# Instance normalisation of 65,536 rows: row statistics by long reductions on two engines, and the last tile in two halves

## The chip, the core and the metric

The kernel runs on one core of one Trainium2 chip. The metric is the device time of one execution in microseconds (us). Executions of the kernel before lie within a few us of one another (5017.2 to 5019.7 in the first series); all runs told here are in the fast state, with a granted clock of 1.0.

Names: VectorE is DVE in the profile, ScalarE is ACT, GpSimd is POOL, and SP issues the transfers. "DMA engine" always means one of the 16 engines of the core that move data; "engine" alone is a compute engine.

## The reference

```python
x: (256, 256, 4096) float32, eps = 1e-5
mean = np.mean(x, axis=2, keepdims=True)
var = np.var(x, axis=2, keepdims=True)
return (x - mean) / np.sqrt(var + eps)
```

That is 65,536 rows of 4096 numbers: 1073.7 MB are read and as much is written.

## The kernel before

A tile is 128 partitions x 4 rows (8.4 MB); there are 128 tiles and three buffers. Each row is reduced by eight bn_stats of 512, and ScalarE normalises it in place. One queue carries loads and stores.

```python
def row(x_tile, r):
    ...
    for j in range(nsub):                       # 8 times
        nc.vector.bn_stats(out=stats[:, j, :], in_=xr[:, r, j, :])
    nc.vector.bn_aggr(out=mv, in_=stats)
    nc.scalar.activation(out=rstd, in_=mv[:, 1:2], func=Sqrt, bias=eps_tile, scale=1.0)
    nc.vector.reciprocal(out=rstd, in_=rstd)
    nc.vector.scalar_tensor_tensor(out=nbias, ...)          # -mean * rstd
    nc.scalar.activation(out=x_tile[:, r, :], in_=x_tile[:, r, :],
                         func=Identity, bias=nbias, scale=rstd)

def finish(i):
    x_tile = tiles.pop(i)
    for r in range(K):
        row(x_tile, r)
    nc.sync.dma_start(out=out_t[i], in_=x_tile)

for i in range(AHEAD):
    load(i)
for i in range(ntiles):
    finish(i)
    if i + AHEAD < ntiles:
        load(i + AHEAD)
```

Of the kernel before, what the change touches and what calls it, by code (L numbers as in the profile page):

```python
# [1 line left out]

# [4 lines left out]


@with_exitstack  # L10
def kernel(
    ctx: ExitStack,
    tc: tile.TileContext,
    x: bass.AP,
    eps: bass.AP,
    out: bass.AP,
):
    nc = tc.nc
    P = 128
    K = 4  # L20
    BUFS = 3
    AHEAD = 2

    x_flat = x.flatten_outer_dims()
    out_flat = out.flatten_outer_dims()
    n, d = x_flat.shape
    ntiles = n // (P * K)
    assert n == ntiles * P * K

    x_t = x_flat.rearrange("(t p k) d -> t p k d", p=P, k=K)  # L30
    out_t = out_flat.rearrange("(t p k) d -> t p k d", p=P, k=K)

    FMAX = nc.vector.BN_STATS_FMAX
    nsub = d // FMAX
    assert d == nsub * FMAX

    io = ctx.enter_context(tc.tile_pool(name="io", bufs=BUFS))
    small = ctx.enter_context(tc.tile_pool(name="small", bufs=8))
    singles = ctx.enter_context(tc.tile_pool(name="singles", bufs=1))

    eps_tile = singles.tile([P, 1], mybir.dt.float32)
    nc.vector.memset(eps_tile, eps)  # L42

    tiles = {}

    def load(i):
        x_tile = io.tile([P, K, d], mybir.dt.float32)
        nc.sync.dma_start(out=x_tile, in_=x_t[i])
        tiles[i] = x_tile

    def row(x_tile, r):
        xr = x_tile.rearrange("p k (s f) -> p k s f", s=nsub)
        stats = small.tile([P, nsub, 6], mybir.dt.float32)
        mv = small.tile([P, 2], mybir.dt.float32)
        rstd = small.tile([P, 1], mybir.dt.float32)
        nbias = small.tile([P, 1], mybir.dt.float32)
        for j in range(nsub):
            nc.vector.bn_stats(out=stats[:, j, :], in_=xr[:, r, j, :])  # L58
        nc.vector.bn_aggr(out=mv, in_=stats)  # L59
        nc.scalar.activation(  # L60
            out=rstd,
            in_=mv[:, 1:2],
            func=mybir.ActivationFunctionType.Sqrt,
            bias=eps_tile,
            scale=1.0,
        )
        nc.vector.reciprocal(out=rstd, in_=rstd)  # L67
        nc.vector.scalar_tensor_tensor(  # L68
            out=nbias,
            in0=mv[:, 0:1],  # L70
            scalar=-1.0,
            in1=rstd,
            op0=mybir.AluOpType.mult,
            op1=mybir.AluOpType.mult,
        )
        nc.scalar.activation(  # L76
            out=x_tile[:, r, :],
            in_=x_tile[:, r, :],
            func=mybir.ActivationFunctionType.Identity,
            bias=nbias,  # L80
            scale=rstd,
        )

    def finish(i):
        x_tile = tiles.pop(i)
        for r in range(K):
            row(x_tile, r)
        nc.sync.dma_start(out=out_t[i], in_=x_tile)

    for i in range(AHEAD):  # L90
        load(i)
    for i in range(ntiles):
        finish(i)
        if i + AHEAD < ntiles:
            load(i + AHEAD)


# [1 line left out]
_INS = ['x', 'eps']  # L99
_OUTS = [((256, 256, 4096), 'float32')]  # L100

_NUMBERS = {'eps': 9.999999747378752e-06}


# [26 lines left out]
```

## Time and profile before

| what | value | how to read it |
|---|---|---|
| time | 5017.97 us, median of 3 | profiled span 5018.0 |
| VectorE, ScalarE busy | 53%, 42% | neither is the bound |
| data queue | 99.7% of 16 DMA engines' span | transfers are the bound |
| one transfer of 8.4 MB | 19.34 us (8 packets of 2418 ns on each DMA engine) | 256 of them are 4951 us, so 67 us of the time are something else |

Columns: queue and kind, packets, MB, share of the 16 DMA engines' span.

```profile
q14 instruction: 61, 0.50, 0.0%
```

Sixty-one packets of 8 KB, rounded to 0.0%. They are the engines' own programs, fetched by the same DMA engines that move the data (the counts and packet times under "The result" show it).

### The profile page before, as it was taken

Reading aid. Unit: us, or ns where it says so; the run is one execution under the profiler, and the core shown is the slowest. Engines: PE = TensorE matmul, PEld = TensorE weight load, DVE = VectorE, ACT = ScalarE, POOL = GpSimd, SP = SyncE. Lnnn points to the kernel's source line nnn. Section 1 sums busy time; section 2 is a strip of 40 time slices with the busy share of each in tenths; the row PEclk is TensorE's granted clock in tenths of the full one; section 3 lists DMA queues with packets and bytes.
Section 4 is the critical chain, followed back from the end, with each engine's and each line's share of the span. In section 5 each row is a group of like instructions: output and inputs, shape, how many; then the busy total and the mean of one; then the engine's idle time right before and its main releaser. Section 6 shows DMA issues by size and latency. Waiting matters only on the chain.

```text
span 5018.0 us, 7844 instructions
## 1 busy us (share of the span) xinstructions
DVE 2667.3 (53%) x5633; ACT 2083.6 (42%) x1025; POOL 0.2 (0%) x4
## 2 busy tenths in 40 slices
DVE  5555455545555455554555545555455544555444
ACT  3444334443444334443344433444334443344433
POOL 0000000000000000000000000000000000000000
DMA  9999999999999999999999999999999999999998
GB/s 426 432 432 432 433 433 434 434 434 433 427 432 429 426 432 430 427 434 427 427 427 432 428 426 433 429 427 429 430 428 427 428 432 427 427 432 428 427 432 362
DMA packets 36925, 2148.00 MB, mean 428 GB/s; under 512 B 4096, under 2 KB 4096, under 8 KB 4096
## 3 DMA queue, kind: packets, MB, share of 16 engines
q1 hardware_dynamic: 36864, 2147.50, 99.7%
q14 instruction: 61, 0.50, 0.0%
HBM read 1073.74 MB, written 1073.74 MB: 428 GB/s over the span
## 4 chain that ended last, share of the span: by engine, by line
DVE 45%; another core or an unknown queue 43%; ACT 9%; DMA 1%; issue 1%; ACTq 0%
DVE stats L58 41%; ACT x_tile L76 9%; DVE mv L59 2%; DMA x_tile<-in_x_dram 1%; DVE rstd L67 1%; DVE nbias L68 1%; ACT rstd L60 1%; ACTq L60 0%
## 5 line engine op out<-in xcount | busy, mean ns | idle before, releaser
L58 DVE BATCH_NORM_STATS2 stats<-x_tile 128x6 f32<-128x512 f32 x4096 | 2506.3, 674 | 2228.2 <-DMA x_tile<-in_x_dram 2228.2
L76 ACT ACTIVATE x_tile<-x_tile,nbias,rstd 128x4096 f32<-128x4096 f32 x512 | 1945.7, 3800 | 403.5 <-DVE nbias L68 403.5
L60 ACT ACTIVATE rstd<-mv,eps_tile 128x1 f32<-128x1 f32 x512 | 148.8, 291 | 2508.5 <-DVE mv L59 2483.6
L59 DVE BATCH_NORM_AGGREGATE mv<-stats 128x2 f32<-128x48 f32 x512 | 183.7, 359 | 4.4
L67 DVE RECIPROCAL rstd<-rstd 128x1 f32<-128x1 f32 x512 | 74.8, 146 | 87.5 <-ACT rstd L60 87.3
L68 DVE SCALAR_TENSOR_TENSOR nbias<-mv,rstd 128x1 f32<-128x1 f32 x512 | 75.2, 147 | 4.3
L60 ACT ACT_TABLE_LOAD x1 | 1.3, 1283 | 0.7 <-PEq L112 0.7
L42 DVE MEMSET eps_tile<- 128x1 f32 x1 | 0.1, 59 | 0.8 <-PEq L112 0.8
L112 POOL MEMSET const-bfloat16-1.0<- 128x1 bf16 x1 | 0.1, 103 | 0.0
L112 POOL MEMSET const-uint8-127<- 128x1 uint8 x1 | 0.1, 102 | 0.0
L112 POOL MEMSET const-float32-0.0<- 128x1 f32 x1 | 0.1, 100 | 0.2 <-issue 0.2
L112 POOL MEMSET const-float32-1.0<- 128x1 f32 x1 | 0.1, 99 | 0.0
## 6 DMA issues: line engine op xcount, KB each, us to landing
x_tile<-in_x_dram SPq DMA_DIRECT2D x128, 52.3
out_dram<-x_tile SPq DMA_DIRECT2D x128, 33.3
```

The costliest lines, as they stand in the source:

```text
L42: nc.vector.memset(eps_tile, eps)
L58: nc.vector.bn_stats(out=stats[:, j, :], in_=xr[:, r, j, :])
L59: nc.vector.bn_aggr(out=mv, in_=stats)
L60: nc.scalar.activation(out=rstd, in_=mv[:, 1:2], func=mybir.ActivationFunctionType.Sqrt, bias=eps_tile, scale=1.0,)
L67: nc.vector.reciprocal(out=rstd, in_=rstd)
L68: nc.vector.scalar_tensor_tensor(out=nbias, in0=mv[:, 0:1], scalar=-1.0, in1=rstd, op0=mybir.AluOpType.mult, op1=mybir.AluOpType.mult,)
L76: nc.scalar.activation(out=x_tile[:, r, :], in_=x_tile[:, r, :], func=mybir.ActivationFunctionType.Identity, bias=nbias, scale=rstd,)
L112: nc = _bacc.Bacc("TRN2", target_bir_lowering=False, num_devices=1)
```

## The change

The intent: fewer and longer instructions for the statistics (VectorE sums a row, ScalarE sums the squares of x minus mean, both normalise), a fixed order of instructions, and a shorter end, since the last tile is loaded, computed and stored in two halves.

```diff
-        for j in range(nsub):
-            nc.vector.bn_stats(out=stats[:, j, :], in_=xr[:, r, j, :])
-        nc.vector.bn_aggr(out=mv, in_=stats)
...
+        def mean(r):
+            row = x_tile[:, r, :].rearrange("p (c f) -> p c f", c=C)      # C = 64
+            tensor_reduce(out=part[:, r, :], in_=row, op=ALU.add)
+            tensor_reduce(out=nsum[:, c], in_=part[:, r, :], op=ALU.add, negate=True)
+            tensor_scalar_mul(out=nmean[:, c], in0=nsum[:, c], scalar1=1.0 / d)
+        def square(r):
+            nc.scalar.activation(out=junk, in_=x_tile[:, r, :], func=AF.Square,
+                                 bias=nmean[:, c], scale=1.0, accum_out=ss[:, c])
+        def scales(c):    # Sqrt on ScalarE; reciprocal and nbias on VectorE
+        def apply_dve(r): # tensor_scalar(row, rstd, nbias, mult, add), 3 rows of 4
+        def apply_act(r): # activation Identity, 1 row of 4
...
-    for i in range(AHEAD):
+    spans = [(t * P * K, K) for t in range(n // (P * K) - 1)]
+    spans += [(n - P * K, K // 2), (n - P * K // 2, K // 2)]
...
+    for i in range(BUFS):
         load(i)
-    for i in range(ntiles):
-        finish(i)
-        if i + AHEAD < ntiles:
-            load(i + AHEAD)
+    for i in range(last + 1):
+        compute(i)
+        if i == last - 2:
+            load(last)
+        store(i)
+        if 1 <= i < last - 2:
+            load(i + 2)
```

More of the change, by code (lines that the diff above doesn't have):

```diff
@@ L18 @@
     nc = tc.nc
+    keep = tc.keep_in_program_order
+    fp32 = mybir.dt.float32
+    AX = mybir.AxisListType
+    AF = mybir.ActivationFunctionType
+    ALU = mybir.AluOpType
     P = 128
@@ L21 @@
     BUFS = 3
-    AHEAD = 2
+    C = 64
     x_flat = x.flatten_outer_dims()
@@ L26, with rows @@
     n, d = x_flat.shape
-    ntiles = n // (P * K)
-    assert n == ntiles * P * K
-    x_t = x_flat.rearrange("(t p k) d -> t p k d", p=P, k=K)
-    out_t = out_flat.rearrange("(t p k) d -> t p k d", p=P, k=K)
-    FMAX = nc.vector.BN_STATS_FMAX
-    nsub = d // FMAX
-    assert d == nsub * FMAX
+    assert n % (P * K) == 0 and d % C == 0
+    spans = [(t * P * K, K) for t in range(n // (P * K) - 1)]
+    spans += [(n - P * K, K // 2), (n - P * K // 2, K // 2)]
+    last = len(spans) - 1
+    def rows(flat, span):
+        r0, k = span
+        return flat[r0 : r0 + P * k, :].rearrange("(p k) d -> p k d", k=k)
@@ L37 @@
     io = ctx.enter_context(tc.tile_pool(name="io", bufs=BUFS))
-    small = ctx.enter_context(tc.tile_pool(name="small", bufs=8))
+    small = ctx.enter_context(tc.tile_pool(name="small", bufs=4))
     singles = ctx.enter_context(tc.tile_pool(name="singles", bufs=1))
-    eps_tile = singles.tile([P, 1], mybir.dt.float32)
+    psum = ctx.enter_context(tc.tile_pool(name="psum", bufs=1, space=bass.MemoryType.PSUM))
+    eps_tile = singles.tile([P, 1], fp32)
     nc.vector.memset(eps_tile, eps)
+    junk = psum.tile([P, d], fp32)
@@ L44 @@
     tiles = {}
     def load(i):
-        x_tile = io.tile([P, K, d], mybir.dt.float32)
-        nc.sync.dma_start(out=x_tile, in_=x_t[i])
+        x_tile = io.tile([P, K, d], fp32)
+        keep(nc.sync.dma_start(out=x_tile[:, : spans[i][1], :], in_=rows(x_flat, spans[i])))
         tiles[i] = x_tile
-    def row(x_tile, r):
-        xr = x_tile.rearrange("p k (s f) -> p k s f", s=nsub)
-        stats = small.tile([P, nsub, 6], mybir.dt.float32)
-        mv = small.tile([P, 2], mybir.dt.float32)
-        rstd = small.tile([P, 1], mybir.dt.float32)
-        nbias = small.tile([P, 1], mybir.dt.float32)
-        for j in range(nsub):
-            nc.vector.bn_stats(out=stats[:, j, :], in_=xr[:, r, j, :])
-        nc.vector.bn_aggr(out=mv, in_=stats)
-        nc.scalar.activation(
-            out=rstd,
-            in_=mv[:, 1:2],
-            func=mybir.ActivationFunctionType.Sqrt,
-            bias=eps_tile,
-            scale=1.0,
-        )
-        nc.vector.reciprocal(out=rstd, in_=rstd)
-        nc.vector.scalar_tensor_tensor(
-            out=nbias,
-            in0=mv[:, 0:1],
-            scalar=-1.0,
-            in1=rstd,
-            op0=mybir.AluOpType.mult,
-            op1=mybir.AluOpType.mult,
-        )
-        nc.scalar.activation(
-            out=x_tile[:, r, :],
-            in_=x_tile[:, r, :],
-            func=mybir.ActivationFunctionType.Identity,
-            bias=nbias,
-            scale=rstd,
-        )
@@ L84, in finish, with compute @@
-    def finish(i):
-        x_tile = tiles.pop(i)
-        for r in range(K):
-            row(x_tile, r)
-        nc.sync.dma_start(out=out_t[i], in_=x_tile)
-    for i in range(AHEAD):
-        load(i)
-    for i in range(ntiles):
-        finish(i)
-        if i + AHEAD < ntiles:
-            load(i + AHEAD)
+    def compute(i):
+        x_tile = tiles[i]
+        k = spans[i][1]
+        part = small.tile([P, K, C], fp32)
+        nsum = small.tile([P, K], fp32)
+        nmean = small.tile([P, K], fp32)
+        ss = small.tile([P, K], fp32)
+        std = small.tile([P, K], fp32)
+        rstd = small.tile([P, K], fp32)
+        nbias = small.tile([P, K], fp32)
+        def mean(r):
+            c = slice(r, r + 1)
+            row = x_tile[:, r, :].rearrange("p (c f) -> p c f", c=C)
+            keep(nc.vector.tensor_reduce(out=part[:, r, :], in_=row, axis=AX.X, op=ALU.add))
+            keep(nc.vector.tensor_reduce(out=nsum[:, c], in_=part[:, r, :], axis=AX.X, op=ALU.add, negate=True))
+            keep(nc.vector.tensor_scalar_mul(out=nmean[:, c], in0=nsum[:, c], scalar1=1.0 / d))
+        def square(r):
+            c = slice(r, r + 1)
+            keep(
+                nc.scalar.activation(
+                    out=junk, in_=x_tile[:, r, :], func=AF.Square, bias=nmean[:, c], scale=1.0, accum_out=ss[:, c]
+                )
+            )
+        def scales(c):
+            keep(nc.scalar.activation(out=std[:, c], in_=ss[:, c], func=AF.Sqrt, bias=eps_tile, scale=1.0 / d))
+            keep(nc.vector.reciprocal(out=rstd[:, c], in_=std[:, c]))
+            keep(nc.vector.tensor_mul(out=nbias[:, c], in0=nmean[:, c], in1=rstd[:, c]))
+        def apply_dve(r):
+            c = slice(r, r + 1)
+            row = x_tile[:, r, :]
+            keep(
+                nc.vector.tensor_scalar(
+                    out=row, in0=row, scalar1=rstd[:, c], scalar2=nbias[:, c], op0=ALU.mult, op1=ALU.add
+                )
+            )
+        def apply_act(r):
+            c = slice(r, r + 1)
+            row = x_tile[:, r, :]
+            keep(nc.scalar.activation(out=row, in_=row, func=AF.Identity, bias=nbias[:, c], scale=rstd[:, c]))
+        for r in range(k - 1):
+            mean(r)
+            square(r)
+        mean(k - 1)
+        scales(slice(0, k - 1))
+        square(k - 1)
+        for r in range(k - 2):
+            apply_dve(r)
+        scales(slice(k - 1, k))
+        apply_dve(k - 1)
+        apply_act(k - 2)
@@ L99, with store @@
+    def store(i):
+        keep(nc.sync.dma_start(out=rows(out_flat, spans[i]), in_=tiles.pop(i)[:, : spans[i][1], :]))
+    for i in range(BUFS):
+        load(i)
+    for i in range(last + 1):
[5 more added lines that the diff above has]
+            load(i + 2)
 _INS = ['x', 'eps']
```

## The prediction

> **What bounds the kernel now.** I began with the page: the engines' busy shares against the DMA queue's.
>
> ```profile
> DVE 2667.3 (53%) x5633; ACT 2083.6 (42%) x1025; POOL 0.2 (0%) x4
> ...
> DMA packets 36925, 2148.00 MB, mean 428 GB/s; under 512 B 4096, under 2 KB 4096, under 8 KB 4096
> ...
> q1 hardware_dynamic: 36864, 2147.50, 99.7%
> ```
>
> VectorE works for half of the span, ScalarE for less, and the one data queue for 99.7%. The best slices of the page move 434 GB/s and the last only 362, so whatever is not full speed lies mostly at the end. The page's chain of work is no help: it gives 45% to VectorE and 43% to "another core or an unknown queue", because it walks back through the statistics of a tile and doesn't see that the transfers run on beside them.
>
> Next, the timeline of one steady period, to see whether transfers wait for computing or the reverse.
>
> ```profile
> 4918.19 0.33 SPq L88 DMA_DIRECT2D out_dram<-x_tile  x1
> 4918.61 0.38 SPq L48 DMA_DIRECT2D x_tile<-in_x_dram  x1
> 4931.53 5.44 DVE L58 BATCH_NORM_STATS2 stats<-x_tile 128x6 f32<-128x512 f32 x9 [17.21 <-DMA x_tile<-in_x_dram]
> ...
> 4956.97 39.79 SPq L88 DMA_DIRECT2D out_dram<-x_tile  x2
> ```
>
> The store of a tile and the load two tiles on are issued together at 4918.2. VectorE had by then waited since 4914.3 for the next tile, which lands at 4931.5; 25.4 us later (4956.97) that tile is stored. So when computing ends, the queue still has 13 to 14 us of an older load to move. This is the slack of the kernel: a tile could take up to 13 us longer to compute before the last DMA engine ran dry. The landing times fit a queue that is served in order: 33.3 us for a store is the 14 us left over plus one transfer of 19.3 us, and 52.3 us for a load is one transfer more.
>
> Then the records of single packets. Each transfer is 8 packets of 64 KB on each of 16 engines; 29,786 of 32,768 took 2418 ns (so 19.34 us for 8), the mean is 2442 ns, and the excess is in the last packet of a transfer. The 16 completions of one transfer lie 0.5 us apart in the first transfer, 6.5 in the 21st, 12 in the 61st, and 11 to 12.7 from there on: one engine falls behind until the leading ones reach the end of their queue as the next store is issued. From transfer 60 on all need some 19.56 us a transfer. The time of the program is that of its slowest engine, 256 transfers, plus the time in which that engine has nothing to do.
>
> Where is that? Windows over the end (columns: busy time of VectorE, ScalarE and GpSimd, clock, DMA share, GB/s):
>
> ```profile
> 4976.00:4980.00 4.00, 4.00 (x10) 2.31 (x2) 0.00 (x0) 1.00 0.34 147
> 4980.00:4984.00 4.00, 4.00 (x10) 3.00 (x3) 0.00 (x0) 1.00 0.26 115
> 4984.00:4988.00 4.00, 4.00 (x9) 3.18 (x2) 0.00 (x0) 1.00 0.08 33
> 4988.00:4996.00 8.00, 3.82 (x10) 7.39 (x3) 0.00 (x0) 1.00 0.00 0
> 4996.00:5016.00 20.00, 0.00 (x0) 0.40 (x1) 0.00 (x0) 1.00 0.97 419
> ```
>
> The last tile is being computed, with nothing left to move. Most engines stop near 4978; a share of 0.08 is about one engine of 16, and the packet records have that last one finish at 4989.8. The last store is issued at 4996.4 and its first packet starts at 4997.3. So the leading engines lose 19 us, the one that counts loses 4997.3 - 4989.8 = 7.4 us.
>
> **What the Trainium skill says.** "DMA: Bandwidth & Descriptors", section "Where 436 GB/s comes from", gives a ceiling of 435.2 GB/s for a core's 16 ports; the trace agrees, with 434 in its best slices and 64 KB per 2418 ns, or 433.7 GB/s for 16. Even 2147.5 MB at 435.2 GB/s would take 4934 us, 1.7% less than now: 2% faster is out of reach for any change that moves the same bytes. The same page, section "Queues, rings and completion order", says that each DMA engine takes its descriptors in ring order; the 33.3 and 52.3 us above agree. "VectorE: DVE Perf Modes", section "The perf-mode tier table", has tensor_reduce at one element a cycle and fp32 tensor_scalar in SBUF at two (1227 ns for 2048). The kernel before has neither, so this stands untested; its bn_stats of 512 take 674 ns, one element per 1/0.96 ns plus 141 ns. "ScalarE: Activation LUTs", section "What ACT_TABLE_LOAD costs", gives 280 ns + 0.833 ns per element for an ACTIVATE with a pointer as bias and 93 ns for a second pointer: 3785 ns at 4096, where the trace has 3800.
>
> **The change, part by part.** Removed from a tile: 32 bn_stats of 674 ns, 4 aggregates, 4 square roots, 4 pairs of small operations. Added, as estimates:
> - A row's sum: one reduce of 4096, 4096/0.96 + 141 = 4.41 us; a reduce of 64, 0.21; a scaling, 0.15 (the small operations before took 0.147). With 0.04 us between dependent ones and some 0.07 overlap between free ones, 4.77 us a row, 19.1 for four.
> - Square of a row on ScalarE: 280 + 3412 = 3.69 us, four times, beside the sums of the next row. The accumulated output may add some 0.1 us.
> - Normalising a row: VectorE 1.227 + 2048/2/0.96 = 2.29 us, three rows; ScalarE 3.80, one row.
>
> VectorE: 4 x 4.77 + 3 x 2.29 + 0.6 = 26.6 us a tile (before 20.8); ScalarE 4 x 3.7 + 3.8 + 0.6 = 19.2 (before 16.3). Both stay well under the 39.2 us that the two transfers of a tile take, so all this work is beside the transfers. "Long instructions" save nothing on the path: VectorE gets more work, not less.
>
> What could touch the path is the latency of a tile. Sums end at 19.1; scales of three rows 19.5; two rows normalised 24.0; scales of the last row 24.4; last row 26.7. On ScalarE the fourth square ends at 22.9, its root at 23.3, the third row at 27.1. So 27.1 us against 25.4: the slack falls from about 14 to 12.3 us and stays positive. The store of a tile is issued 1.7 us later and the leading engines run into it at a smaller spread, some 10 instead of 12 us, so the slow phase (19.56 instead of about 19.47 us a transfer of the slowest engine) begins perhaps 20 transfers sooner: 20 x 0.09, about +2 us.
>
> The start: the built order of issues is the same in both kernels. Three loads are already issued together at 0.73 us before (the scheduler had moved the third up), then store 0, store 1, load 3. So the extra load ahead in the source changes nothing. A second table load (1.28 us, once) falls in tile 0, whose store queues behind load 2 until about 62 us anyway. Tile 1 should be done at 22.6 + 2 x 27.1 + about 2 = 79 us, just before the first store has left the queue at some 82.
>
> The end: the order becomes store 125, half load, half load, store 126, half store, half store. On the slowest engine, from the landing of tile 126: store 125 to 19.4, the halves to 29.1 and 38.8, store 126 to 58.2, half stores to 67.9 and 77.6. Tile 126 is done at 27.1; a half needs 9.5 (two sums) + 3.7 + 0.4 + 3.8 = 17.5 us, so the first half, landed at about 31, is done by 49, the second by 65 to 66. The last store thus joins a queue that is busy until 67.9: no gap. Before, the same count gives 85.4. Saved: about 7.5 us, which is the gap of 7.4 measured above.
>
> Sum: 5018.0 - 7.4 + 2 = about 5012; I put 5011, since the earlier slow phase is the softest term.
>
> **The rivals.** First, VectorE's normalisation runs at one element a cycle, 4.41 us. Then a tile takes 33 us and the slack is about 6. Steady state would still be bound by transfers, but tile 1 would be done only at about 90 us, 8 us after the first store leaves the queue, the last half would be 1 to 3 us late, and the spread would hit its limit much sooner (some 8 us). Time: 5018 - 7 + 8 + 2 + 8, about 5029. For it speaks only that this trace has no such instruction; against it the table of the skill. Second, engines that run dry cost more than I count: the excess of packets goes from 3 ns a packet at 700 us to some 29 after 1250 us, as the spread reaches its limit. If a tighter slack raises it by another 10 ns, that is 2048 x 10 ns = 20 us, about 5031. Third, reading the windows as "the queue is idle from 4978 to 4997" would promise 19 us and 4999; I hold against it that the lagging engine carries its delay to the end, so that the last stores of the new kernel should end spread over several us. It would come true if shorter transfers let that engine catch up. Fourth, computing becomes the bound: it would take a tile of over 39 us, which no term gives.
>
> **Range and chances.** Most weight is on 5008 to 5016. The gap's 19 us taken whole gives the lower end, 5001; the first or second rival gives the upper, 5028. Faster by 2% (below 4917.6) is beneath the time at the port ceiling: 0.01. Slower by 2% (above 5118) needs 0.8 us more for each tile: 0.02. Within 2%: 0.97.
>
> **What would show it.** Right: the queue again at 99.7% or more; VectorE near 68% and ScalarE near 49% busy; long reduces near 4.4 us, normalisation near 2.3; a tile's store some 27 us after its landing; DMA share without a zero in windows before the last store, and completions of the last store microseconds apart. Wrong: normalisation of 4.4 us, a gap near 82 us, a share below 0.97 in middle windows, mean packets well above 2442 ns, or a last half done after the queue is empty.

## The result

The changed kernel took **4995.92 us** (median of 4: 4990.08 to 4996.78) against 5018.83 us for the kernel before in the same rounds. The ratio is 0.9952 (95% interval 0.9935 to 0.9969). Ratios here are the mean time of one kernel's fast runs over that of the other's of the same rounds, so they are not quite the ratio of the medians. The prediction was 5011, with a range down to 5001.

The page of the changed kernel, first its engines and queues:

```profile
DVE 3392.6 (68%) x2436; ACT 2501.4 (50%) x1413; POOL 0.2 (0%) x4
...
q1 hardware_dynamic: 37152, 2147.50, 99.9%
q14 instruction: 38, 0.31, 0.0%
```

VectorE works 725 us more and the kernel is faster all the same: transfers are still the bound. VectorE executes 2436 instructions instead of 5633, and the instruction queue has 38 packets in place of 61.

The costliest groups (line, engine, operation, operands, shapes, count, busy us, mean ns, idle time before them):

```profile
L74 DVE TENSOR_REDUCE part<-x_tile 128x64 f32<-128x4096 f32 x512 | 2258.8, 4412 | 1520.3 <-DMA x_tile<-in_x_dram 1520.3
...
L95 DVE TENSOR_SCALAR x_tile<-x_tile,rstd,nbias 128x4096 f32<-128x4096 f32 x383 | 912.6, 2411 | 10.4 <-DVE nbias L89 1.1
...
L81 ACT ACTIVATION_READ_ACCUMULATOR junk<-x_tile,nmean 128x1 f32 x512 | 95.5, 187 | 0.0
```

The long reduce takes 4412 ns and the normalisation 2411 ns, so VectorE does run the latter at about two elements a cycle. The accumulated output of Square costs an instruction of its own of 187 ns.

One steady period of the timeline, which answers to the one shown of the kernel before:

```profile
4862.97 0.33 SPq L118 DMA_DIRECT2D out_dram<-x_tile  x1
4863.35 0.43 SPq L57 DMA_DIRECT2D x_tile<-in_x_dram  x1
4875.38 4.42 DVE L74 TENSOR_REDUCE part<-x_tile 128x64 f32<-128x4096 f32 x1 [12.47 <-DMA x_tile<-in_x_dram]
...
4902.43 0.33 SPq L118 DMA_DIRECT2D out_dram<-x_tile  x1
```

A tile takes 4902.43 - 4875.38 = 27.05 us, where 27.1 was expected, and 12.4 us of queue are left when a store is issued.

Windows over the end (columns as in the prediction):

```profile
4940.00:4960.00 20.00, 13.73 (x12) 12.39 (x8) 0.00 (x0) 1.00 1.02 416
4960.00:4970.00 10.00, 9.83 (x9) 5.38 (x5) 0.00 (x0) 1.00 0.98 426
4970.00:4976.00 6.00, 2.00 (x4) 5.97 (x4) 0.00 (x0) 1.00 0.85 366
4976.00:4980.00 4.00, 0.81 (x1) 1.67 (x1) 0.00 (x0) 1.00 0.73 311
4980.00:4984.00 4.00, 0.00 (x0) 0.00 (x0) 0.00 (x0) 1.00 0.93 401
```

The zero of the kernel before is gone. Only the leading DMA engines pause near 4976, and the 16 completions of the last store lie 4.6 us apart. So the end went as predicted, and what is missing from the prediction came from the middle. Here are windows over the middle, first before, then after; the last two columns are the DMA share and GB/s.

```profile
250.00:1125.00 875.00, 469.78 (x994) 371.36 (x183) 0.00 (x0) 1.00 1.00 433
1125.00:2000.00 875.00, 461.63 (x974) 357.93 (x176) 0.00 (x0) 1.00 1.00 430
2000.00:3000.00 1000.00, 538.64 (x1139) 422.82 (x208) 0.00 (x0) 1.00 1.00 429
```

```profile
250.00:1125.00 875.00, 598.43 (x431) 442.54 (x251) 0.00 (x0) 1.00 1.00 433
1125.00:2000.00 875.00, 597.66 (x428) 436.36 (x246) 0.00 (x0) 1.00 1.00 434
2000.00:3000.00 1000.00, 677.37 (x486) 499.10 (x282) 0.00 (x0) 1.00 1.00 431
```

Before, the rate falls from 433 to 430 after 1125 us; after, it holds 434 until 2000. The DMA share says 1.00 throughout: a slower packet counts as a busy one.

The packet records tell where the slower packets come from. I followed the completion of the last of the 16 DMA engines from transfer to transfer and subtracted 19.32 us. Before the leaders run out of queue, this excess is zero in most transfers and jumps in a few. Each column here is a packet of the instruction queue, with the excess of the last DMA engine in the transfer during which it ran. These are the fetches in VectorE's rhythm from 491 us before and from 1117 us after, and the others from 971 us after (the rhythm is explained below):

```
before: fetch at us   491.5  601.2  720.0  836.7  953.4  1062.9
        excess us      0.66   0.71   0.78   0.78   0.76    0.78
after:  fetch at us  1116.8 1349.5 1582.3 1853.7 2086.5
        excess us      0.82   0.93   0.94   0.96   0.94
after, other fetches  971.3 1151.6 1495.1 1809.5 2156.4
        excess us      0.00   0.00   0.00   0.00   0.00
```

Before, the jumps come every 110 to 117 us, which is the time in which VectorE executes some 128 instructions; after, every 230 to 270. The fetch packet itself takes 0.31 us, and in every case the data packet that starts 0.3 us after it is 0.15 to 0.65 us longer than 2418 ns. At 720.0 us, for instance, that packet takes 2886 ns: 0.31 + 0.47 is the jump of 0.78. The others have a longer packet after them too, but on a DMA engine that isn't the last, so the excess stays zero. Three earlier fetches in VectorE's rhythm after the change (340.7, 614.2 and 845.4 us) cost only 0.32, 0.00 and 0.60 us: their DMA engine was not yet, or only just, the last one. And not every jump is a fetch: in the first 40 transfers of the changed kernel there are others of up to 1.1 us. The count fits too. The trace records 5639, 1663 and 520 instructions on VectorE, ScalarE and SP before; at 128 for a packet that is 44 + 13 + 4 = 61. After it is 2568, 1928 and 399: 20 + 15 + 3 = 38. Both are exactly the packets of the queue.

So the theory to test (F) is: **every 128 instructions of a compute engine take some 0.8 to 0.9 us from one particular DMA engine. VectorE's program always falls on the same one, which therefore becomes the last, and the last one sets the time.** Long instructions help by being few. By F, 24 or 25 fetches fewer should give some 17 us beside the 7.4 of the end. The rivals: (T) the two halves win all 19 us of idle time at the end instead of 7.4; (L) the longer latency of a tile holds the DMA engines closer together.

### The profile page after: what moved, and what is told of

Read it like the earlier page. It is cut to its first block, busy times and chain, and to the rows that moved or that the text cites. A ratio compares the mean times of both kernels' runs of the same rounds, so it can differ in the third digit from the quotient of the medians.

```text
span 4994.1 us, 4917 instructions
## 1 busy us (share of the span) xinstructions
DVE 3392.6 (68%) x2436; ACT 2501.4 (50%) x1413; POOL 0.2 (0%) x4
## 3 DMA queue, kind: packets, MB, share of 16 engines
q1 hardware_dynamic: 37152, 2147.50, 99.9%
## 4 chain that ended last, share of the span: by engine, by line
DVE 53%; DMA 23%; another core or an unknown queue 20%; ACT 3%; issue 1%; SPq 0%; ACTq 0%
DVE part L74 37%; DMA x_tile<-in_x_dram 22%; DVE x_tile L95 12%; DVE nsum L75 2%; ACT junk L81 2%; ACT x_tile L103 2%; DVE nmean L76 1%; DMA out_dram<-x_tile 1%; DVE nbias L89 1%; DVE rstd L88 0%; SPq L118 0%; ACTq L159 0%; ACT L87 0%; ACT std L87 0%
## 5 line engine op out<-in xcount | busy, mean ns | idle before, releaser
L74 DVE TENSOR_REDUCE part<-x_tile 128x64 f32<-128x4096 f32 x512 | 2258.8, 4412 | 1520.3 <-DMA x_tile<-in_x_dram 1520.3
L81 ACT ACTIVATE junk<-x_tile,nmean 128x4096 f32<-128x4096 f32 x512 | 1883.0, 3678 | 2445.2 <-DVE nmean L76 2445.2
L95 DVE TENSOR_SCALAR x_tile<-x_tile,rstd,nbias 128x4096 f32<-128x4096 f32 x383 | 912.6, 2411 | 10.4 <-DVE nbias L89 1.1
L103 ACT ACTIVATE x_tile<-x_tile,nbias,rstd 128x4096 f32<-128x4096 f32 x129 | 488.5, 3787 | 0.1
L75 DVE TENSOR_REDUCE nsum<-part 128x1 f32<-128x64 f32 x512 | 112.7, 220 | 17.7
L81 ACT ACTIVATION_READ_ACCUMULATOR junk<-x_tile,nmean 128x1 f32 x512 | 95.5, 187 | 0.0
L76 DVE TENSOR_SCALAR nmean<-nsum 128x1 f32<-128x1 f32 x512 | 78.7, 154 | 17.5
L87 ACT ACTIVATE std<-ss,eps_tile 128x3 f32<-128x3 f32 (+1 forms) x258 | 76.2, 295 | 8.3
L88 DVE RECIPROCAL rstd<-std 128x3 f32<-128x3 f32 (+1 forms) x258 | 41.6, 161 | 8.6 <-ACT std L87 8.6
L89 DVE TENSOR_TENSOR nbias<-nmean,rstd 128x3 f32<-128x3 f32 (+1 forms) x258 | 41.5, 161 | 8.9
```

Source lines behind the costliest of these rows:

```text
L74: keep(nc.vector.tensor_reduce(out=part[:, r, :], in_=row, axis=AX.X, op=ALU.add))
L75: keep(nc.vector.tensor_reduce(out=nsum[:, c], in_=part[:, r, :], axis=AX.X, op=ALU.add, negate=True))
L76: keep(nc.vector.tensor_scalar_mul(out=nmean[:, c], in0=nsum[:, c], scalar1=1.0 / d))
L81: nc.scalar.activation(out=junk, in_=x_tile[:, r, :], func=AF.Square, bias=nmean[:, c], scale=1.0, accum_out=ss[:, c])
L87: keep(nc.scalar.activation(out=std[:, c], in_=ss[:, c], func=AF.Sqrt, bias=eps_tile, scale=1.0 / d))
L88: keep(nc.vector.reciprocal(out=rstd[:, c], in_=std[:, c]))
```

## The experiments

Three calls of four kernels each, with the kernel before in the same rounds of each call (c0 to e3, e4 to e7, c1 to f3). "Against before" is the ratio times that kernel's mean (5021.8, 5019.9 and 5019.7 us), less that mean. One per mille is 5 us, and the 95% intervals are 1.2 to 1.5 per mille wide on each side, so two runs less than some 6 to 9 us apart are not told apart. The second call has no control of the changed kernel; there, and where runs of different calls are compared, the comparison goes through the kernel before. The page and packet records of a run are those of one execution.

| run | what | median us | ratio (95%) | against before | VectorE's fetches, all fetches |
|---|---|---|---|---|---|
| c0_after_again | changed kernel | 5005.12 | 0.9965 (0.9950 to 0.9979) | -17.6 | 20, 38 |
| e1_tail | before, halves only | 5014.44 | 0.9983 (0.9970 to 0.9995) | -8.5 | 44, 61 |
| e2_notail | changed, no halves | 5011.57 | 0.9982 (0.9970 to 0.9994) | -9.0 | 20, 38 |
| e3_pad_dve | changed + 19 VectorE memsets a tile | 5018.98 | 0.9994 (0.9982 to 1.0006) | -3.0 | 39, 57 |
| e4_pad_pool | changed + 19 GpSimd memsets, not paced | 5017.39 | 1.0000 (0.9986 to 1.0014) | 0 | 20, 57 |
| e5_pad_dve_100 | changed + 100 VectorE memsets | 5079.68 | 1.0118 (1.0105 to 1.0132) | +59 | 121, 139 |
| e6_latency | changed, tile 4.7 us longer | 5033.89 | 1.0028 (1.0015 to 1.0040) | +14 | 22, 40 |
| e7_lean | changed, fewer VectorE instructions | 4970.99 | 0.9905 (0.9892 to 0.9919) | -48 | 12, 30 |
| c1_after_control | changed kernel | 4996.34 | 0.9953 (0.9941 to 0.9965) | -23.6 | 20, 38 |
| f1_pool_paced | changed + 19 GpSimd instructions, paced | 5002.02 | 0.9957 (0.9943 to 0.9972) | -21.6 | 21, 59 |
| f2_lean_pad8 | lean + 8 VectorE memsets | 4993.60 | 0.9948 (0.9936 to 0.9960) | -26 | 20, 38 |
| f3_lean_halfstore | lean, stores in halves | 4975.81 | 0.9913 (0.9901 to 0.9926) | -44 | 12, 33 |

(VectorE's fetches are its recorded instructions over 128; all fetches are the packets of the instruction queue in that run's page, of which GpSimd has 19 and 20 in e4 and f1.) All results were correct.

**c0_after_again**, the changed kernel unedited, as a control:

> Control on the chip of this call. All theories: 4990 to 4997 us (first runs: 4990.1 to 4996.8). Traces so far: 61 instruction fetches of 8 KB before, 38 after; the last of the 16 DMA engines steps back by 0.7 to 0.95 us in just the transfers that hold a fetch of VectorE's stream. Fetch theory (F): VectorE's 5633 instructions at 64 bytes are 44 fetches before, 2436 are 19 after, and 25 fewer at some 0.7 us are the 16 to 17 us that the tail's 7.4 us do not explain.

The median, 5005, is outside what all theories expected. The runs took 4993 to 5015 us, so this chip scatters more than the first did (the kernel before: 5014 to 5026). The medians of different calls can't be compared here, and what follows uses ratios within a call.

**e1_tail**: the kernel before with only the end of the change.

```diff
+    spans = [... all tiles but the last ..., half, half]
-        nc.sync.dma_start(out=out_t[i], in_=x_tile)
+        if i == last - 2:
+            load(last)
+        keep(nc.sync.dma_start(out=rows(out_flat, spans[i]), in_=x_tile[:, : spans[i][1], :]))
```

> The kernel before with only the last tile in two halves. F: only the 7.4 us gap of the slowest DMA engine goes, fetches stay at about 61, so 5010 to 5012 us. Tail rival (T: the halves let the late engine catch up and win the whole 19 to 23 us): 4995 to 4999. Latency rival (L: the gain beyond the gap comes from the longer latency of a tile in the new statistics, which holds the engines closer together): also 5010 to 5012, so this run separates T from F and L.

It gains 8.5 us, and 61 packets stay in the instruction queue. That is the gap of the last DMA engine (7.4 us), not the 19 us of the leaders, so T falls.

**e2_notail**: the rest of the change alone.

```diff
-    spans = [(t * P * K, K) for t in range(n // (P * K) - 1)]
-    spans += [(n - P * K, K // 2), (n - P * K // 2, K // 2)]
+    spans = [(t * P * K, K) for t in range(n // (P * K))]
```

> The changed kernel with the last tile whole. F and L: the new statistics keep their share, the gap at the end comes back: 4995.9 + 7 to 9 = 5003 to 5005 us, 38 fetches. T: about 5018.

It gains 9.0 us. The two halves of the change add up to 17.5, just what the control gained. So the statistics win time of their own, although VectorE works longer in them. But 9.0 is about half of the 17 us that F asks for; the interval (3 to 15 us) doesn't reach it. In the traced execution, its slowest (5021.8 us), transfers with a fetch lost 20.6 us, near the control's 17.4; what was larger was the loss in the other transfers (some 37 against 20 us), a part that F does not explain.

**e3_pad_dve**: VectorE's instruction count up again, in the time when it waits for the next tile.

```diff
+        for j in range(PAD):          # PAD = 19, after the last normalisation of a tile
+            keep(nc.vector.memset(scratch[:, j : j + 1], 0.0))
```

> The changed kernel with 19 memsets of 128x1 on VectorE after each tile's last normalisation (some 1.2 us of the 12 us in which VectorE waits for the next tile; the latency of the tile does not change). Writes only scratch. F: 2451 more VectorE instructions are 19 more fetches at 0.7 to 0.9 us on the same DMA engine: 4996 + 13 to 17 = 5009 to 5013 us, about 57 fetches. L and T: unchanged, 4990 to 4998.

14.6 us of the control's 17.6 are lost again, as F expected and neither rival did (the time itself, 5019, is above F's 5009 to 5013, as the control is above its own). Little else changed: VectorE's busy time rose by 32 us of 3393, and in the packet records transfers with a fetch lost 35.2 us where the control lost 17.4. Its page:

```profile
DVE 3424.4 (68%) x4887; ACT 2501.3 (50%) x1413; POOL 0.2 (0%) x4
...
q14 instruction: 57, 0.47, 0.0%
```

**e4_pad_pool**: the same memsets on GpSimd.

```diff
-            keep(nc.vector.memset(scratch[:, j : j + 1], 0.0))
+            keep(nc.gpsimd.memset(scratch[:, j : j + 1], 0.0))
```

> The same 19 memsets a tile, now on GpSimd: the same number of instructions and about the same number of fetches (57) as with the padding on VectorE. F, in the form that each engine's instruction stream is fetched by its own DMA engine: GpSimd's 19 fetches delay another DMA engine by no more than VectorE's 19 delay theirs, so 4994 to 5000 us. If all fetches fell on one DMA engine or slowed all: 5009 to 5013, as with VectorE. Latency rival: unchanged, 4990 to 4998.

It came out as slow as the padding on VectorE, but the timeline shows that it doesn't answer its question:

```profile
0.73 6.25 POOL L120 MEMSET scratch<- 128x1 f32 x188 [0.29 <-POOLq L150]
...
81.88 9.90 DVE L98 TENSOR_SCALAR x_tile<-x_tile,rstd,nbias 128x4096 f32<-128x4096 f32 x1
...
109.75 2.93 POOL L120 MEMSET scratch<- 128x1 f32 x87 [3.63 <-issue]
```

The memsets waited for nothing, and all of them ran within 113 us, with all their 19 fetches in the first transfers. There the last DMA engine lost 15.5 us more over the first eight transfers than in the control (20.7 against 5.2 us, counted as above). Not all of this is fetches. While the memsets ran, VectorE's normalisation of a row took up to 9.90 us in place of 2.41, so the second store was issued only at 91.8, and from 90.0 to 92.7 us no data packet ran: 2.7 of the 15.5 us. That leaves some 0.7 us for each of the 19 fetches, as an estimate. f1 below is the mended form.

**e5_pad_dve_100**: a larger dose of e3 (PAD = 100).

> 100 memsets a tile on VectorE (some 6 us, still within its 12 us of waiting). F: 12,900 more instructions are 101 more fetches at 0.7 to 0.9 us: 4996 + 70 to 91 = 5066 to 5087 us (the line through the 19-memset run should hit it). Latency rival: unchanged, 4990 to 5000.

```profile
DVE 3674.4 (72%) x15336; ACT 2501.5 (49%) x1413; POOL 0.2 (0%) x4
...
q14 instruction: 139, 1.14, 0.1%
```

59 us slower than the kernel before, and within what F expected. From e3 to e5 VectorE's fetches go from 39 to 121 and the times from -3 to +59 us: 62 / 82 = 0.76 us a fetch. The line in the page still reads only 0.1%.

**e6_latency**: a longer tile, with almost the same instruction count.

```diff
+        for _ in range(2):
+            row = x_tile[:, k - 1, :]
+            keep(nc.vector.tensor_scalar_mul(out=row, in0=row, scalar1=1.0))
```

> The changed kernel with the last row multiplied by 1.0 twice more on VectorE before the store: a tile takes 27.0 + 4.8 = 31.8 us, only 2 more instructions (2 fetches in all). F: the slowest DMA engine still has 12 - 5 = 7 us of queue left when the store is issued, so 4996 + 2 = 4995 to 5001 us; the spread of the completions is capped some 5 us lower. Latency rival L (a longer tile holds the engines together and gains): below 4990. My second rival of the prediction (a tighter slack costs some 20 us): 5010 to 5020.

This is a miss for F's number: +14 us against before, some 35 us worse than the changed kernel, and more than the second rival's 5010 to 5020 too. It shows that latency is not harmless, and it refutes L, which wanted a gain. Two places in its timeline, and one window near the end (columns as in the prediction):

```profile
55.03 31.82 SPq L121 DMA_DIRECT2D out_dram<-x_tile  x2
86.91 0.42 SPq L57 DMA_DIRECT2D x_tile<-in_x_dram  x1
```

```profile
2034.12 4.62 DVE L118 TENSOR_SCALAR x_tile<-x_tile 128x4096 f32<-128x4096 f32 x2
2038.81 0.33 SPq L121 DMA_DIRECT2D out_dram<-x_tile  x1
```

```profile
5010.00:5012.00 2.00, 1.61 (x3) 2.00 (x2) 0.00 (x0) 1.00 0.00 0
```

At the start, the second store is issued only at about 86.5 (the two stores are merged in one line), after the first one has left the queue: over the first eight transfers the last DMA engine lost 8 us more than in c0. In the steady part, the leaders reach the end of their queue at transfer 30 instead of 84, and the last DMA engine lost 60.6 us over the rest, against 37.9 in c0. That steady part, 23 us, is the second rival of the prediction, at its own size of some 20 us. The end adds a third part: the second half of the last tile, made longer as well, is ready only after the queue is empty, and no packet runs from 5011.1 to 5018.7 us, which is 7.6 us. 8 + 23 + 7.6 is the 38.4 us by which this trace is longer than c0's.

**e7_lean**: still fewer instructions on VectorE.

```diff
-            keep(nc.vector.tensor_reduce(out=part[:, r, :], in_=row, axis=AX.X, op=ALU.add))
-            keep(nc.vector.tensor_reduce(out=nsum[:, c], in_=part[:, r, :], ..., negate=True))
-            keep(nc.vector.tensor_scalar_mul(out=nmean[:, c], in0=nsum[:, c], scalar1=1.0 / d))
+            keep(nc.vector.tensor_reduce(out=nsum[:, c], in_=x_tile[:, r, :], ..., negate=True))
-    func=AF.Square, bias=nmean[:, c], scale=1.0, ...
+    func=AF.Square, bias=nsum[:, c], scale=float(d), ...          # (d x - sum)^2
-    func=AF.Sqrt, bias=eps_tile, scale=1.0 / d
+    func=AF.Sqrt, bias=eps_tile, scale=1.0 / d**3
-    nc.vector.tensor_mul(out=nbias, in0=nmean, in1=rstd)
+    nc.vector.scalar_tensor_tensor(out=nbias, in0=nsum, scalar=1.0 / d, in1=rstd, mult, mult)
```

> The changed kernel with the mean's small instructions removed: one reduce of 4096 per row straight to the negated sum, ScalarE squares 4096 x - sum, and the divisions are folded into the root and the last multiplication. VectorE has 11 instructions a tile in place of 19, ScalarE 11 as before. Latency about 25.6 us. F: 8 fewer fetches of VectorE at 0.7 to 0.9 us: 4996 - 6 = 4987 to 4992 us. Latency rival L: a shorter tile lets the engines drift further, 5000 or more.

```profile
DVE 3204.2 (64%) x1412; ACT 2501.3 (50%) x1413; POOL 0.2 (0%) x4
```

4970.99 us, 48 us less than the kernel before and the fastest of all. The sign is F's, but the size isn't: about 6 us were expected beyond the changed kernel, and it was 24 to 30.

**c1_after_control**: the changed kernel again, for the third call.

> Control on the chip of this call, 4990 to 5008 us by the two series so far; the next three are read against it.

4987 to 5006 us, -23.6 us against before.

**f1_pool_paced**: e4 mended.

```diff
+        keep(nc.gpsimd.tensor_copy(out=scratch[:, 0:1], in_=nbias[:, k - 1 : k]))
+        for j in range(1, PAD):       # PAD = 19
+            keep(nc.gpsimd.memset(scratch[:, j : j + 1], 0.0))
```

> The GpSimd padding again, mended: in the first try all 2432 memsets ran in the first 113 us, since they waited for nothing, and cost 15 us there. Now the first of the 19 in a tile copies that tile's nbias, so they are paced by the tiles. Fetch theory with one DMA engine for each instruction stream: GpSimd's 19 fetches fall on another DMA engine than VectorE's and delay it no more, so the control plus 0 to 5 us. If what counts is the number of fetches of the whole core (61 before, 57 here, 38 in the control): the control plus 13 to 17 us, as with the padding on VectorE.

```profile
DVE 3463.8 (69%) x2436; ACT 2501.3 (50%) x1413; POOL 139.5 (3%) x2455
...
q14 instruction: 59, 0.48, 0.0%
```

With 59 fetches, almost as many as in the kernel before, it is 2 us from its control by ratio (the medians are 5.7 apart); the same number of extra instructions on VectorE cost 14.6. The times alone would only just tell these apart; the packet records are firmer. At VectorE's fetches (575, 808, 1041, 1312 us) the last DMA engine steps back by 0.85 to 0.95 us, and at those that come in between at GpSimd's pace (621, 892, 1125, 1396) by 0.00. So GpSimd's program falls on another DMA engine, which had time to spare.

**f2_lean_pad8**: is it the instruction count that makes the lean kernel fast, or its shorter tile?

```diff
+        for j in range(PAD):          # PAD = 8, on the lean kernel
+            keep(nc.vector.memset(scratch[:, j : j + 1], 0.0))
```

> The lean kernel (4971 us, 30 us better than the changed kernel's, where 6 were expected) with 8 memsets a tile on VectorE after the last normalisation: as many VectorE instructions and fetches as the changed kernel (38), but a tile still takes some 25.5 us instead of 27. If the fetches alone made the lean kernel fast: near the control, 4990 to 5005. If the shorter tile (more queue left when the store is issued, so that the leading engines run dry later) made it: 4971 to 4976. If both: in between, 4978 to 4988.

4993.6 us, by ratio the same as the changed kernel. Eight memsets of 59 ns, while VectorE waits anyway, take back all that the lean kernel had won over the changed one. So it was the count, not the latency.

**f3_lean_halfstore**: more queue ahead of the DMA engines.

```diff
         for r in range(k - 2):
             apply_dve(r)
+        if k > 2:
+            store(i, 0, k - 2)        # rows 0 and 1 now, rows 2 and 3 at the end
```

> The lean kernel with each tile's store in two halves, rows 0 and 1 issued as soon as VectorE has normalised them, some 3 us before the tile is done. If running dry of the leading engines costs time (the lean kernel took 68 ns a transfer above 19.32 us before they ran dry at transfer 140, 116 after): they run dry later or never, 4960 to 4967 us. If it costs nothing: 4971 plus up to 5 us for 127 more transfers' completions. It should beat both kernels either way.

4975.8 us: no gain over the lean kernel. By its packet records the excess above the usual packet did fall, from 9.1 ns on 64 KB packets to 7.8 and 1.0 ns on packets of 64 and 32 KB, or from 18 to 10 us for each DMA engine. But a packet of 32 KB usually takes 1213 ns, so two of them are 8 ns more than one of 64 KB; with 1032 such pairs on each DMA engine that gives 8 us back.

## Why the prediction was right or wrong

**Right: the bound.** Transfers bound both kernels; 725 us more work on VectorE did not make the kernel slower.

**Right: the end.** The prediction gave 7.5 us, from the gap of the last DMA engine, and against the 19 us of the windows. The halves alone gained 8.5 (e1). The prediction's third rival, 4999 us, lies nearer to the measured 4996 than its own 5011, but for a reason that e1 rules out: a right number isn't a right cause.

**Right: the latency.** 27.1 us expected, 27.05 measured; the normalisation at two elements a cycle (2.29 expected, 2.41 measured), so the first rival did not come. Every sign that the prediction listed for being right came true (queue 99.9%, VectorE 68%, ScalarE 50%, no zero before the last store, completions 4.6 us apart), and none of them could show the term that was missing.

**Wrong: the step "'Long instructions' save nothing on the path: VectorE gets more work, not less".** It looked at the time of instructions and forgot that they must be fetched: the sum has no term for 24 fetches fewer. The statistics alone gained 9.0 us (e2), and the whole change gained 17.6 to 24, where the prediction's sum has 6. In the two first traces, the account for the last DMA engine is as follows: transfers with a fetch lost 32.4 us before and 17.2 after, the others 21.9 and 23.1 (both from transfer 8 on), the first eight transfers are 3.5 us shorter, and the gap at the end 7.4. That makes -15.2 + 1.2 - 3.5 - 7.4 = -24.9 us, for a measured difference of 4994.1 - 5018.0 = -23.9.

**Wrong: the term of +2 us for a slow phase that begins 20 transfers sooner.** The limit of the spread fell as predicted, from about 12 to 10 us. But the leaders first reached the end of their queue at transfer 98 of the changed kernel (84 and 72 in its two controls), not at about 40, while before it was 58. The trace of e2, whose program is the same up to the last tile, has it at 46, so one execution doesn't settle it. The drift towards the limit had been taken as given. In fact a good part of it is made by fetches, and VectorE's had become fewer than half: from transfer 8 to that point, 6.2 us of 7.4 fell in transfers with a fetch before, and 4.6 of 9.8, 5.8 of 8.4 and 4.4 of 9.0 in the three traces of the changed kernel. The rest has no cause shown.

**Its second rival was real**, but for another kernel: less queue in hand costs some 20 us in the steady part where a tile takes 4.7 us longer (e6). What the change's own 1.7 us cost was not measured alone; it may be why e2 gained less than the fetches promise. **Its range** did not hold its own rivals: their sums are 5029, 5031 and 4999, and it ran from 5001 to 5028.

**What stays open.** The price of a fetch isn't constant: 0.76 us from 39 to 121 fetches, about 0.8 to 1 from 20 to 39, but about 3 us each from 12 to 20 (e7 against the changed kernel; f2 shows that the count does it). In the traces of f2 and e7, 6 us of their difference are in transfers with a fetch and 9 in those without one (e7's trace is of its slowest execution, so 7 us of the difference of the medians are not in it); the latter is excess that grows once the leaders have caught up with their queue (transfer 98 in f2, 140 in e7). Why packets are slower then was not settled: f3 kept more queue and halved the excess, but at a price that hid what it was worth. Open, too, is why the changed kernel scatters by up to 22 us between executions of one call and the lean one by 8. The traces say where: c0's and c1's are 13.3 us apart, with 17.4 and 18.8 us lost in transfers with a fetch and some 20 and 31 in the others. And extra instructions were tried on VectorE and GpSimd only, not on ScalarE.

## What to carry to other kernels

In a kernel bound by transfers, like this one, instructions cost twice: in the engine's time, which is hidden as long as a tile is ready well before the queue runs dry (e6 shows the limit), and in the DMA engines' time, which is not, as each 128 of them are one more packet on a DMA engine that also moves data. So read the instruction queue's packet count even where its share rounds to 0.0%, and write fewer instructions for the engine that has the most; the lean form did so and beat both kernels, at 4971 us. And judge a gap by the last of the 16 DMA engines, not by their mean share.

## What the Trainium skill lacked or had wrong

- "Runtime: NRT & Kernel Launch", section "Instruction fetch mechanics", has programs refilled in blocks of 16 KiB (256 instructions), with a cost that is "mostly hidden". Here the packets are 8 KB, one for each 128 recorded instructions (61 and 38 in all), and in a kernel bound by transfers they are not hidden: 0.66 to 0.96 us of the last DMA engine for each of VectorE's in the table above, and 62 us for 82 of them in e3 and e5.
- "DMA: Bandwidth & Descriptors", section "Queues, rings and completion order", lists row 14 as runtime-internal without saying that instruction fetches on it delay the data of one DMA engine: the data packet after a fetch is up to 0.65 us longer than its 2418 ns. Nor does a page say that different engines' programs fall on different DMA engines, as f1 shows for GpSimd and VectorE (2 us against 14.6 for the same padding).
- "VectorE: DVE Perf Modes", section "The perf-mode tier table", proved right in kind: 4412 ns for the reduce of 4096 and 2411 ns for the normalisation, 5% over the prediction's estimate of 2.29 us made from it.
